# Moving sums of a pooling mixer: VectorE's additions in SBUF, or accumulating transfers in DRAM

## The chip, the cores and the metric

The kernel runs on one core of a Trainium2 chip. A core has TensorE (PE, matrix products; its weight loads are shown as PEld), VectorE (DVE), ScalarE (ACT), GpSimd (POOL) and SyncE (SP), which work from queues of their own and wait for one another by semaphores. SyncE, ScalarE and GpSimd also issue DMA transfers, which sixteen DMA engines carry out. The metric is device microseconds (us) of one execution; lower is better.

## What is computed

The reference is one decoder block on x (1024 tokens x 1024 channels, float32): an RMSNorm and one projection into pooling inputs u, attention's q, k, v, and gates; a multi-scale pooling branch and a sliding-window attention branch, each projected and multiplied by its sigmoid gate, added, projected by W_o, normalised and added to x; and then an MLP with a squared ReLU. What the change touches is the pooling. Its 512 channels are four groups of 128, with windows of 2, 4, 8 and 16 tokens:

```
for gi, w in enumerate((2, 4, 8, 16)):
    c = cs[..., gi * 128:(gi + 1) * 128]          # running sums of u over the tokens
    upper = c[:, 1:]
    lower = jnp.pad(c[:, :S + 1 - w], ((0, 0), (w - 1, 0), (0, 0)))
    count = jnp.minimum(t + 1, w)
    pooled.append((upper - lower) / count)
diff = pooled - u                                  # group by group
mixed = einsum('bsgc,gcd->bsgd', diff, w_pool)
y_pool = mixed * pool_scale
```

So for each token t and channel: the mean of the last w values of u (fewer for the first w - 1 tokens), minus u itself.

## The kernel before

The kernel works in stages, each of which streams weights from DRAM and keeps TensorE at products of 128x128 by 128x512 blocks. Operands are float32, split by a helper (`split`, lines 99 to 104) into a high part (ScalarE's cast, line 101) and a low part (VectorE's subtraction, line 104); each product is three passes over these parts (line 32). The stages in order of time:

1. Projection to q, k, v and attention, block by block of 128 tokens (to about 166 us). In the gaps of the attention's matmuls a generator (`others`, line 633) runs the projection to u. For each group gi, in the order 3, 2, 1, 0, two halves of u are formed (`u_half`, line 591), and u[gi], 128 channels x 1024 tokens, is stored to DRAM (line 611). In the same stage GpSimd makes small tiles for the attention (lines 295 to 330) and, for each of the eight token blocks, two accumulating transfers of the attention's output into DRAM (line 424).
2. Gates (about 166 to 319 us): a Strassen-like scheme of seven block products (class `Pairs`, line 461). In its first part eight pairs of gate weights get two products each (`first` and `second`, lines 847 to 853); weights arrive by line 475, are split by lines 101 and 104, and are multiplied at line 511. Meanwhile the operands for the second part are built from x (`load_x` and `build_gate`, lines 727 to 748). In the second part (line 902) the other products follow and the gates are stored to DRAM.
3. Branches (about 319 to 406 us): first eight calls of `branch` for the attention's projection (line 975), then eight for the pooling's (line 994). Within the first eight, after m = 2, 3, 5 and 6, `pool_part` prepares the pooling groups 1, 0, 2 and 3.
4. W_o (GpSimd's accumulating loads of line 966 add blocks of it), the norms, and the MLP up and down (to the end).

`pool_part(gi)` (line 934) loads u[gi] into an SBUF tile, calls `pool_in` (line 685) and splits the result into the operands `yphi` and `yplo` that the second eight branches multiply. `pool_in` adds the bias on ScalarE (line 688); then VectorE forms the moving sum by doubling: sums over 2 tokens from u and u shifted by one, sums over 4 from those shifted by two, and so on (line 692), with a small copy for the first columns (line 693); 1, 2, 3 and 4 additions for the four groups, each into a further tile of the pool `yy`, which has four buffers. Line 696 forms sum / w minus u, and lines 697 and 698 mend the first w - 1 columns, where the count is smaller.

The order of the work: in the regions `manual_schedule` (lines 755 and 859) the engines that are named there issue in the order of the program; these are TensorE, VectorE and ScalarE, in the second region SyncE too. GpSimd's queue everywhere, and SyncE's outside the second region, are ordered by a scheduler at build time, which lets a later instruction of a queue go ahead of an earlier one when it reckons that the earlier isn't ready. Semaphores are put in by the framework: a transfer that reads what another one wrote waits, in the queue of the engine that issues it, until the other has landed.

Of the kernel before, what the change touches and what calls it, by code (L numbers as in the profile page):

```python
# [8 lines left out]
F32 = mybir.dt.float32  # L9
F32R = mybir.dt.float32r  # L10
AF = mybir.ActivationFunctionType
ALU = mybir.AluOpType
AX = mybir.AxisListType

P = 128
S = 1024
# [5 lines left out]
WINDOWS = (2, 4, 8, 16)  # L22
# [16 lines left out]
C_CNT = C_SIN + NT * 8  # L39
# [3 lines left out]
V_BU = V_G + 8  # L43
# [7 lines left out]
def block_kernel(ctx: ExitStack, tc, xt, x, consts, vecs, sinks, b_qkv, g_post, g_mlp_post,  # L51
                 w_qkv, w_u, w_g, w_pool, w_bp, w_ba, w_o, w_up, w_dn, x1_dram, spill, y_dram, wbp_dram, f_dram, r_dram, out):
    nc = tc.nc
    act, dve, pool, pe = nc.scalar, nc.vector, nc.gpsimd, nc.tensor
# [8 lines left out]
    psum = {"pool": psa_pool.__enter__(), "bufs": {"sc": 1, "at": 3, "mm": 3}}  # L63

    z_dram, u_dram = (spill[i:j] for i, j in ((0, 16), (16, 20)))
    cnt = [0]

    def nm(s):
        cnt[0] += 1
        return f"{s}_{cnt[0]}"  # L70
# [22 lines left out]
    def flat(t):  # L93
        return t.rearrange("p a b -> p (a b)")
# [4 lines left out]
    def split(hi, lo, src, eng=dve, first=None):  # L99
        if first is None:  # L100
            act.copy(hi, src)  # L101
        else:
            first.tensor_copy(hi, src)
        eng.tensor_tensor(lo, src, f32(hi), ALU.subtract)  # L104
# [42 lines left out]
    cst = cp.tile([P, C_N], F32, name="cst")  # L147
    vec = cp.tile([P, V_N], F32, name="vec")
# [533 lines left out]
                return  # L682
            owed[0] -= c

    def pool_in(gi, u, place):

        w = WINDOWS[gi]
        act.activation(u, u, AF.Identity, bias=vec[:, V_BU + gi:V_BU + gi + 1])
        src, step = u, 1
        while step < w:  # L690
            t = place()
            dve.tensor_tensor(t[:, step:], src[:, step:], src[:, :S - step], ALU.add)
            dve.tensor_copy(t[:, :step], src[:, :step])
            src, step = t, 2 * step
            yield
        dve.scalar_tensor_tensor(u[:, w - 1:], src[:, w - 1:], 1.0 / w, u[:, w - 1:], ALU.mult, ALU.subtract)
        dve.tensor_tensor(src[:, :w - 1], src[:, :w - 1], cst[:, C_CNT:C_CNT + w - 1], ALU.mult)
        dve.tensor_tensor(u[:, :w - 1], src[:, :w - 1], u[:, :w - 1], ALU.subtract)
        yield

    def y_place():
        return flat(yy.tile([P, 2, 512], F32, tag="y", name=nm("t")))
# [139 lines left out]

    NG0, NHELD = 8, 6

    def first(p):
# [86 lines left out]
    def pool_part(gi):  # L934
        u = yy.tile([P, S], F32, tag="y", name=nm("d"))
        nc.sync.dma_start(u, u_dram[gi])
        for _ in pool_in(gi, u, y_place):
            pass
        hi = xp.tile([P, S], F32R, tag="x", name=nm("yphi"))
        lo = xp.tile([P, S], F32R, tag="x", name=nm("yplo"))  # L940
        split(hi, lo, u)
        ysp[gi] = hi, lo
# [32 lines left out]
    for m in range(8):  # L975
        branch(w_ba[m], lambda k, hl, th: asp[th][k // 2][hl][:, k % 2, :], 8, m)
        if m == 4:
            sums = wo_load((1, 0), a32, zg[8, 2][1])
            wo_add(sums, (1, 1))
        if m in (2, 3, 5, 6):  # L980
            pool_part({2: 1, 3: 0, 5: 2, 6: 3}[m])
# [363 lines left out]
    def acc4(name):  # L1345
        return [dl.tile([P, 512], F32, tag="acc", name=nm(name), bufs=16) for _ in range(4)]
# [91 lines left out]
    u, v, c11, c12 = acc4("u"), acc4("v"), acc4("c11"), acc4("c12")  # L1438
# [124 lines left out]
```

## Time and profile before

| | us |
|---|---|
| median of 3 runs | 1110.14 (1108.49 to 1111.05) |
| the profiled execution | 1109.43 |
| its span in the trace | 1107.6 |
| TensorE busy | 1097.7 (99%) |
| VectorE busy | 807.1 (73%) |
| ScalarE busy | 547.6 (49%) |
| GpSimd busy | 62.7 (6%) |
| granted TensorE clock | 0.998 |
| DMA, mean over the span | 184 GB/s |

How to read the rows below: L692 is line 692 of the kernel; an arrow `t<-d` means that tile t is written from tile d; `x4` counts instructions. In a view of an engine's instructions in order of time, the first number is the start and the second the length in us, and the brackets at the end hold the idle time before it and what ended that. In a view of waits the numbers are the us in total, the times, and the longest. In a table of stretches come, after the stretch and its length, the busy us of PE, PEld, DVE, ACT and POOL with their instructions, then the granted clock, the mean busy share of the DMA engines, and GB/s. SPq and ACTq are the instructions of SyncE and ScalarE that issue a DMA. Rows of DMA queues give packets, MB and the share of the sixteen engines' time; rows of DMA issues give count, size of one, and us from issue to landing. `spill_dram` is the DRAM tensor that holds the gates (z, 16 slots) and u (4 slots).

### The profile page before, as it was taken

The numbers are of one execution on the slowest core, as the hardware profiler recorded it, in microseconds if no ns is written. First come the engines' busy times: TensorE is split into PE (matmuls) and PEld (weight loads), VectorE is DVE, ScalarE is ACT, GpSimd is POOL, SyncE is SP. The second block draws the span as 40 slices with busy tenths as digits, with TensorE's granted clock in tenths as the row PEclk, the third lists the DMA queues.
The fourth block names the chain that finished last, engine by engine and source line by source line (L and its number), as shares of the span: only waits on it lengthen the run. The fifth ranks groups of instructions, "written<-read, shape, count | busy, mean of one in ns | idle before, by whom it ended". The sixth has DMA issues, their size and how long they took to land.

```text
span 1107.6 us, 13855 instructions
## 1 busy us (share of the span) xinstructions
PE 1097.7 (99%) x5108; PEld 907.5 (82%) x5108; DVE 807.1 (73%) x1175; ACT 547.6 (49%) x916; POOL 62.7 (6%) x107
## 2 busy tenths in 40 slices
PE   9999999999999999999999999999999999999997
PEld 7888788888888888878888888888888888888886
DVE  5578867899768796899878867666548944456596
ACT  7466656444432337587555654444434434344342
POOL 0344220000001120000000000000000000000000
PEclk9999999999999999999999999999999999999999
DMA  9406578355677581570457645445597535534673
GB/s 349 161 11 137 149 169 278 132 191 209 224 256 246 152 186 58 192 271 32 162 197 264 242 169 199 146 151 199 178 371 232 189 98 174 177 102 152 204 229 119
DMA packets 89747, 203.71 MB, mean 184 GB/s; under 512 B 8400, under 2 KB 21072, under 8 KB 89680
## 3 DMA queue, kind: packets, MB, share of 16 engines
q1 hardware_dynamic: 77536, 176.88, 48.0%
q10 hardware_dynamic: 5616, 19.66, 4.6%
q0 software_dynamic: 6528, 6.29, 4.0%
q8 instruction: 40, 0.66, 0.3%
q14 instruction: 27, 0.22, 0.1%
HBM read 147.23 MB, written 55.58 MB: 183 GB/s over the span
## 4 chain that ended last, share of the span: by engine, by line
PE 88%; DVE 5%; DMA 3%; ACT 2%; issue 2%; DVEq 0%; SPq 0%; ACTq 0%
PE mm L511 24%; PE at L511 16%; PE at L1406 16%; PE mm L1406 12%; PE mm L601 4%; PE mm L187 3%; PE mm L445 2%; PE at L196 1%; PE at L419 1%; PE mm L447 1%; PE sc L355 1%; PE sc L187 1%; DMA d<-spill_dram 1%; PE at L1048 1%; PE mm L1048 1%
## 5 line engine op out<-in xcount | busy, mean ns | idle before, releaser
L1406 PE MATMUL at<-ar,wh 128*128 128x512 f32 x744 | 169.6, 389 | 0.0
L1406 PEld LDWEIGHTS at<-ar,wh 128*128 128x128 f32 x744 | 139.6, 188 | 29.3 <-DVE ar L104 0.4
L104 DVE TENSOR_TENSOR wh<-raw,wh 128x1024 fp32r<-128x1024 f32 x53 | 64.8, 1223 | 99.4 <-ACT wh L101 99.4
L1406 PE MATMUL mm<-ar,wh 128*128 128x512 f32 x576 | 131.0, 389 | 0.0
L101 ACT CAST wh<-raw 128x1024 fp32r<-128x1024 f32 x53 | 55.8, 1053 | 146.7 <-PE at L1406 71.6
L1406 PEld LDWEIGHTS mm<-ar,wh 128*128 128x128 f32 x576 | 108.1, 188 | 22.4
L101 ACT CAST wh<-st 128x512 fp32r<-128x512 f32 (+1 forms) x97 | 61.6, 646 | 74.4 <-PE at L511 19.9
L104 DVE TENSOR_TENSOR wh<-st,wh 128x512 fp32r<-128x512 f32 (+1 forms) x97 | 68.8, 719 | 27.8 <-ACT wh L101 25.3
L511 PE MATMUL mm<-gr,wh 128*128 128x512 f32 x333 | 80.4, 391 | 0.0
L511 PEld LDWEIGHTS mm<-gr,wh 128*128 128x128 f32 x333 | 62.1, 188 | 13.1 <-DVE gr L1087 0.4
L511 PE MATMUL mm<-T,wx 128*128 128x512 f32 x288 | 67.6, 389 | 0.0
L511 PEld LDWEIGHTS mm<-T,wx 128*128 128x128 f32 x288 | 54.1, 188 | 11.2
L511 PE MATMUL at<-T,wx 128*128 128x512 f32 x252 | 59.1, 389 | 0.0
L511 PEld LDWEIGHTS at<-T,wx 128*128 128x128 f32 x252 | 47.3, 188 | 9.8
L511 PE MATMUL mm<-x,wh 128*128 128x512 f32 x240 | 55.2, 389 | 0.0
L511 PEld LDWEIGHTS mm<-x,wh 128*128 128x128 f32 x240 | 45.0, 188 | 9.4
L104 DVE TENSOR_TENSOR ar<-B,ar 128x1024 fp32r<-128x1024 f32 x37 | 45.1, 1219 | 4.0 <-ACT ar L101 3.9
L601 PE MATMUL mm<-x,wh 128*128 128x512 f32 x192 | 47.5, 395 | 0.0
L101 ACT CAST ar<-B 128x1024 fp32r<-128x1024 f32 x37 | 38.9, 1051 | 5.9 <-DMA B<-in_w_dn_dram 3.0
L601 PEld LDWEIGHTS mm<-x,wh 128*128 128x128 f32 x192 | 35.3, 188 | 7.7
L511 PE MATMUL at<-gr,wh 128*128 128x512 f32 x150 | 36.7, 390 | 0.0
L101 ACT CAST wx<-ws 128x512 fp32r<-128x512 f32 x30 | 18.6, 620 | 32.7 <-DVE ws L487 17.9
(384 smaller groups left out, 2162.4 us busy)
## 6 DMA issues: line engine op xcount, KB each, us to landing
raw<-f_dram SPq DMA_DIRECT2D x53, 512.0 KB, 3.7
f_dram<-g SPq DMA_DIRECT2D x30, 512.0 KB, 3.3
B<-in_w_dn_dram SPq DMA_DIRECT2D x24, 512.0 KB, 6.3
st<-in_w_up_dram SPq DMA_DIRECT2D x20, 512.0 KB, 4.1
st<-in_w_g_dram SPq DMA_DIRECT2D x18, 512.0 KB, 4.6
f_dram<-g ACTq DMA_DIRECT2D x17, 512.0 KB, 2.6
g<-spill_dram SPq DMA_DIRECT2D x16, 512.0 KB, 5.4
raw<-in_w_dn_dram SPq DMA_DIRECT2D x16, 512.0 KB, 4.7
```

The lines of the kernel that those rows point to most:

```text
L101: act.copy(hi, src)
L104: eng.tensor_tensor(lo, src, f32(hi), ALU.subtract)
L187: pe.matmul(bq, xs_[k][n // 4][:, xh, n % 4 * P:(n % 4 + 1) * P], wq[k][:, h, :], start=k == 0 and j == 0, stop=k == NK - 1 and j == 2)
L196: pe.matmul(bkv_of(n), xs_[k][n // 4][:, xh, n % 4 * P:(n % 4 + 1) * P], wkv[k // 2][:, h, k % 2, :], start=k == 0 and j == 0 and not (joi ...
L355: pe.matmul(sb[:, kv, i, :nk], qt[r, qx, m * P:(m + 1) * P], kx[r, k0:k0 + nk], start=j == 0, stop=j == 2)
L419: pe.matmul(flat(yb), v[:, kv, :], flat(p[:, 4 * kv:4 * kv + 4]), start=j == 0, stop=j == len(mms) - 1)
L445: pe.matmul(bs[th], whi[:, k, :], rhs(k, hl, th), start=k == 0 and hl == 0, stop=False)
L447: pe.matmul(bs[th], wlo[:, k, :], rhs(k, 0, th), start=False, stop=k == nk - 1)
L511: pe.matmul(b, w[:, wh, kt, :], xo[kt][:, xh, :], start=not after and kt == 0 and j == 0, stop=kt == 3 and j == 2, skip_group_check=after)
L601: pe.matmul(b, (whi, wlo)[h][:, k, :], xr(k, xh, th), start=j == 0, stop=j == len(mms) - 1)
L1048: pe.matmul(bs[t], gop[i][kt // 2][gh][:, kt % 2, t * P:(t + 1) * P], wop[i][kt // 2][wh][:, kt % 2], start=not after and kt == 0 and j == ...
L1406: pe.matmul(bs[t], fo[fh][:, k2, t * P:(t + 1) * P], wo_[wh][:, k2, :], start=not after and s2 == 0 and k2 == 0 and j == 0, stop=s2 == NS ...
```

## The change

The moving sums are formed in DRAM. The DRAM tensor gets ten more slots of 128 x 1024, one for each doubling step of each group. Ahead of the gates' stage in the program, `window_sums` issues for every step and group, in GpSimd's queue, a copy of the source (u, or the sum of the step before) into the new slot, and an accumulating transfer that adds the same source to it, shifted by 1, 2, 4 or 8 tokens. `pool_part` loads u and the finished sum. Since the sums are now of u without its bias, `pool_in` scales the first w - 1 columns by w / count (VectorE), then takes sum / w + bias (ScalarE) and subtracts u + bias (VectorE).

```diff
+    sum_dram = [[spill[20 + gi * (gi + 1) // 2 + i] for i in range(gi + 1)] for gi in range(4)]
...
-    def pool_in(gi, u, place):
-
-        w = WINDOWS[gi]
-        act.activation(u, u, AF.Identity, bias=vec[:, V_BU + gi:V_BU + gi + 1])
-        src, step = u, 1
-        while step < w:
-            t = place()
-            dve.tensor_tensor(t[:, step:], src[:, step:], src[:, :S - step], ALU.add)
-            dve.tensor_copy(t[:, :step], src[:, :step])
-            src, step = t, 2 * step
-            yield
-        dve.scalar_tensor_tensor(u[:, w - 1:], src[:, w - 1:], 1.0 / w, u[:, w - 1:], ALU.mult, ALU.subtract)
-        dve.tensor_tensor(src[:, :w - 1], src[:, :w - 1], cst[:, C_CNT:C_CNT + w - 1], ALU.mult)
-        dve.tensor_tensor(u[:, :w - 1], src[:, :w - 1], u[:, :w - 1], ALU.subtract)
-        yield
+    def window_sums(step):
+
+        for gi in (1, 0, 2, 3):
+            if 1 << step < WINDOWS[gi]:
+                src, dst = (sum_dram[gi][step - 1] if step else u_dram[gi]), sum_dram[gi][step]
+                pool.dma_start(dst, src)
+                pool.dma_start(dst[:, 1 << step:], src[:, :S - (1 << step)], accum_op=ALU.add)
+
+    def pool_in(gi, u, t):
+
+        w, bias = WINDOWS[gi], vec[:, V_BU + gi:V_BU + gi + 1]
+        act.activation(u, u, AF.Identity, bias=bias)
+        edge = t[:, :w - 1]
+        dve.scalar_tensor_tensor(edge, edge, float(w), cst[:, C_CNT:C_CNT + w - 1], ALU.mult, ALU.mult)
+        act.activation(t, t, AF.Identity, bias=bias, scale=1.0 / w)
+        dve.tensor_tensor(u, t, u, ALU.subtract)
...
+    for step in range(4):
+        window_sums(step)
+
     NG0, NHELD = 8, 6
...
         nc.sync.dma_start(u, u_dram[gi])
-        for _ in pool_in(gi, u, y_place):
-            pass
+        t = y_place()
+        nc.sync.dma_start(t, sum_dram[gi][-1])
+        pool_in(gi, u, t)
...
-    spill = nc.dram_tensor("spill_dram", (20, P, S), F32, kind="Internal").ap()
+    spill = nc.dram_tensor("spill_dram", (30, P, S), F32, kind="Internal").ap()
```

## The prediction

> **What bounds the kernel now.** I read the page's header first, then the busy time of each engine by stage, then what TensorE waited for.
>
> ```profile
> span 1107.6 us, 13855 instructions
> ...
> PE 1097.7 (99%) x5108; PEld 907.5 (82%) x5108; DVE 807.1 (73%) x1175; ACT 547.6 (49%) x916; POOL 62.7 (6%) x107
> ```
>
> ```profile
> 0.00:20.00 20.00, 18.47 (x89) 15.21 (x90) 10.88 (x21) 13.93 (x25) 0.20 (x4) 1.00 0.88 327
> ...
> 110.00:215.00 105.00, 104.89 (x515) 85.05 (x512) 81.17 (x122) 60.41 (x140) 13.76 (x19) 1.00 0.64 173
> 215.00:320.00 105.00, 105.00 (x464) 86.91 (x463) 87.78 (x131) 45.51 (x59) 0.00 (x0) 1.00 0.65 218
> 320.00:360.00 40.00, 40.00 (x178) 33.11 (x177) 33.92 (x56) 12.03 (x14) 4.16 (x4) 1.00 0.80 259
> 360.00:420.00 60.00, 59.85 (x264) 49.13 (x263) 50.97 (x57) 22.33 (x27) 11.97 (x10) 1.00 0.65 156
> ...
> 1090.00:1108.00 18.00, 10.71 (x48) 8.54 (x46) 10.76 (x32) 2.95 (x9) 0.00 (x0) 0.88 0.31 117
> ```
>
> ```profile
> PEld mm L445 <- ACT wh L101: 0.5, 1, 0.5
> PEld at L511 <- DVE gr L104: 0.5, 1, 0.5
> ```
>
> The columns of the second fence are the stretch, its length, busy time (instructions) of PE, PEld, DVE, ACT and POOL, the granted clock, the DMA share and GB/s. TensorE is idle for 1107.6 - 1097.7 = 9.9 us in all, and 1.5 + 7.3 of that lie at the two ends. From 215 to 360 us, which holds the whole pooling stage, it is idle for 0.00 us, and from 360 to 420 for 0.15. The clock is 1.00 wherever it counts. So the kernel is bound by TensorE, and the other engines show in the time only where they make TensorE wait. The longest such waits around the change are 0.5 us.
>
> **What the change takes away.** The rows of the removed work, and of the operation that ScalarE gets once more for each group:
>
> ```profile
> L692 DVE TENSOR_TENSOR t<-t x6: 1206/1220/1225, 322.4 to 354.7; 128x1022 f32<-128x1022 f32 x3, 128x1020 f32<-128x1020 f32 x2, 128x1016 f32<-128x1016 f32 x1
> L692 DVE TENSOR_TENSOR t<-d x4: 1218/1224/1225, 314.4 to 346.8; 128x1023 f32<-128x1023 f32 x4
> ...
> L688 ACT ACTIVATE d<-d,vec x4: 1150/1152/1153, 313.2 to 345.6; 128x1024 f32<-128x1024 f32 x4
> ```
>
> Ten additions of 1.22 us leave VectorE: 12.2 us, and some small copies with them. The final subtraction stays, in another form. ScalarE gains 4 x 1.15 = 4.6 us, at 12.03 us busy of 40: hidden by its own idle time. VectorE's 12.2 us lie between 314 and 358 us, where TensorE is never idle, so taking them away is worth between 0 and the 0.15 us that TensorE loses after 360. I take 0: the cover is TensorE's own stream, which has no gap to close.
>
> **What it adds.** Ten copies and ten accumulating transfers from DRAM to DRAM, about 512 KB each, in GpSimd's queue, and four loads of 512 KB in SyncE's. An accumulation may go only when its copy has landed, and the next copy of the same group only when the accumulation has; GpSimd waits for each in its own queue. Two questions decide: do the sums come in time, and whom do they disturb?
>
> *In time?* GpSimd's queue, its price for a DMA, and the first and the last of the loads that will need the sums:
>
> ```profile
> 169.38 2.04 POOL L424 DMA_DIRECT2D y_dram<-yt  x2 [9.37 <-ACT qkv L736]
> 350.47 1.72 POOL L959 COPY s<-g 128x1 f32<-128x1 f32 x2 [179.06 <-DVE t L693]
> ```
>
> ```profile
> L966 POOL DMA_DIRECT2D s<-in_w_o_dram x8 | 9.7, 1262 | 15.1 <-DMA s<-in_w_o_dram 7.6 <-DVE wh L104 3.6 <-DVE wo L104 2.1
> ```
>
> ```profile
> s<-in_w_o_dram POOLq DMA_DIRECT2D x8, 512.0 KB, 7.3
> ...
> spill_dram<-u SPq DMA_DIRECT2D x4, 512.0 KB, 3.9
> ```
>
> ```profile
> 308.80 0.33 SPq L936 DMA_DIRECT2D d<-spill_dram  x1
> ...
> 341.47 0.33 SPq L936 DMA_DIRECT2D d<-spill_dram  x1
> ```
>
> GpSimd is free from 171.4 to 350.5 us. No DMA from DRAM to DRAM is in this trace. The nearest rows are the accumulating loads of W_o (1.26 us on GpSimd, 7.3 us to landing), and the store of u (3.9 us) as the low end for a copy. If all twenty ran strictly one after the other from 171.4, each at 1.26 + 7.3 = 8.56 us, the last would land at 171.4 + 171 = 343 us, just after the last group's load goes out now. With the copies at 3.9 it is 309 us. A following copy belongs to another group in most places and needn't wait for the accumulation ahead of it, so it is earlier still. Against lateness there is a little more room behind: these three rows (the third is a piece of the chain of waits, 192 matmuls in 43.52 us) say how much.
>
> ```profile
> 359.13 1.23 DVE L104 TENSOR_TENSOR yplo<-d,yphi 128x1024 fp32r<-128x1024 f32 x1
> ```
>
> ```profile
> 318.89 0.39 PE L445 MATMUL mm<-yahi,wh 128*128 128x512 f32 x1
> ```
>
> ```profile
> 166.30 43.52 PE mm L511 x192
> ```
>
> The last group is ready at 359.13 + 1.23 = 360.4 us. A branch is 24 matmuls of 43.52 / 192 = 0.227 us, so TensorE comes to the second eight branches at 318.89 + 8 x 5.44 = 362.4, and to that group's rows, the last quarter, 4.1 us later. So I take the sums to be in time. The Trainium skill's page "DMA: Bandwidth & Descriptors" (Anatomy of one DMA, SWDGE path) fits 2.0 us plus the bytes at 436 GB/s, 3.2 us for such a transfer; by it, an estimate, the strictly serial chain would be done at 171.4 + 20 x 4.46 = 261 us. The trace's 7.3 us is more than twice that and decides here.
>
> *Whom do they disturb?* First, when they run. GpSimd isn't in the lists of engines with a hand-written order, so the scheduler may place the sums in any gap after u is stored. SyncE shows that it does such things:
>
> ```profile
> 113.49 0.33 SPq L611 DMA_DIRECT2D spill_dram<-u  x1
> ...
> 158.72 0.33 SPq L475 DMA_DIRECT2D st<-in_w_g_dram  x1
> ...
> 163.98 0.33 SPq L475 DMA_DIRECT2D st<-in_w_g_dram  x1
> ...
> 167.62 0.53 SPq L611 DMA_DIRECT2D spill_dram<-u  x1
> ...
> 170.71 0.95 SPq L475 DMA_DIRECT2D st<-in_w_g_dram  x1
> ```
>
> The fourth and last u is written in the program before gate 4 and gate 6 are loaded (the third and fourth L475), yet both loads go out ahead of it. I therefore expect the sums of group 3 from about 113.5 + 3.9 = 117 us on, and the others as their u lands. Now the DMA engines (the last two columns are share and GB/s):
>
> ```profile
> 160.00:170.00 10.00, 10.00 (x46) 8.27 (x45) 7.86 (x12) 5.75 (x10) 0.63 (x3) 1.00 1.02 262
> 170.00:180.00 10.00, 10.00 (x46) 8.29 (x45) 6.62 (x10) 4.80 (x10) 1.41 (x2) 1.00 1.08 313
> 180.00:190.00 10.00, 10.00 (x46) 8.29 (x45) 8.93 (x14) 6.42 (x12) 0.00 (x0) 1.00 0.74 290
> 190.00:200.00 10.00, 10.00 (x46) 8.29 (x45) 8.16 (x14) 5.85 (x10) 0.00 (x0) 1.00 0.32 107
> ```
>
> From 160 to about 184 us they are full before anything is added. What a transfer takes of them comes from the shares of two queues: ScalarE's 16 stores in 215 to 320, and GpSimd's 8 accumulations in 320 to 420:
>
> ```profile
> q10 hardware_dynamic: 2304, 8.39, 21.2%
> ```
>
> ```profile
> q0 software_dynamic: 2176, 4.19, 24.7%
> ```
>
> A plain 512 KB is 0.212 x 105 / 16 = 1.4 us of all 16 engines, an accumulated one 0.247 x 100 / 8 = 3.1 us. A pair is 4.5 us, the ten pairs 45 us. The four extra loads later are 4 x 1.4 us at 0.80 share, with no TensorE wait near them: nothing.
>
> In the full stretch the gate weights come just in time:
>
> ```profile
> 179.39 0.62 ACT L101 CAST wh<-st 128x512 fp32r<-128x512 f32 x1 [3.59 <-DMA st<-in_w_g_dram]
> ```
>
> ```profile
> 180.04 0.69 DVE L104 TENSOR_TENSOR wh<-st,wh 128x512 fp32r<-128x512 f32 x1 [1.53 <-ACT wh L101]
> ```
>
> This is gate 8, loaded at 170.71 and landed at 179.3, 8.6 us later. TensorE's 192 matmuls from 166.30 are sixteen blocks of 2.72 us; gate 8's is the seventh, so it starts at 166.30 + 6 x 2.72 = 182.6, and needs the low part two matmuls later, at 183.1. That part is ready at 180.7. The load may be 2.4 us later; beyond that, each us is one of TensorE's, and TensorE never gets it back. From 160.7 to 179.3 (18.6 us) one chain of pairs, each some 15 us long (two landings of 7.3), takes 4.5 / 15 = 0.30 of the engines: 5.6 us of delay for the loads behind, so 5.6 - 2.4 = **3.2 us of stall**. Bounds: if the sums start only at 171.4, a single copy (1.4 us) lies ahead of the landing, and the stall is 0; if two groups' chains run at once they take 0.5 to 0.6 of the engines, 9.3 us at 0.5, and the stall is 6.9. I take the middle one, because GpSimd waits in order for each landing, which keeps the chains mostly apart. The additions' 0 and the sums' 3.2 make the sum.
>
> Three rows of the DMA queues and issues from 160 to 190 us:
>
> ```profile
> q1 hardware_dynamic: 4493, 8.12, 78.3%
> q0 software_dynamic: 1050, 0.51, 16.1%
> ...
> xr<-in_xt_dram SPq DMA_DIRECT2D x4, 512.0 KB, 9.4
> ```
>
> GpSimd's queue q0 already has a sixth of the engines there, with 0.51 MB in small packets, beside SyncE's q1. The Trainium skill's page "DMA: Bandwidth & Descriptors" (Queues, rings and completion order) says that each DMA engine takes turns between queues packet by packet. By that rule GpSimd's queue would get up to half while it has work, the 6.9 us end. These rows, with q0 not always at work, neither show nor exclude the half.
>
> **The rivals.** (1) *No stall, no change.* The scheduler keeps the sums behind the attention's last transfer, or SyncE's queue isn't slowed enough: 1.4 us of delay against 2.4 us of slack. For it: TensorE rides over landings of 8.6 us already. Against it: SyncE's early loads. Time: 1110.1. (2) *Two chains at once,* with the half share: 6.9 us, 1117. For it: the groups' u come 18 us apart, about a pair's length. (3) *The sums are late.* SyncE then stands at the load of a sum, with the branch weights and gates queued behind it, and TensorE starves. It decides once a DRAM-to-DRAM transfer costs more than 8.56 us in series from 171.4; at the 9.4 us that the x loads take in the full stretch, 20 x 10.66 = 213 us end at 385, 43 us after the last load goes now, and about 37 us of stall less what overlaps: some 20, 1130. Against it: most copies overlap, and the start is early. (4) *Faster by more than 0.2%.* VectorE would have to hold TensorE somewhere after 360 that the waits don't show; at most 0.15 us is there, and only a luckier order downstream gives 2.2 us: 1107.5.
>
> **How the numbers follow.** The three runs span 2.6 us; about 0.2%, 2.2 us, is what a measurement of this kernel can tell from no change. The profiled execution took 1109.43 us for its span of 1107.6; plus 3.2 that is 1112.6. The runs' median is 0.7 above it, so 1113.3. Chances: forecast 0.42, rival (1) 0.38, (2) 0.10, (3) 0.05, (4) 0.05. The range goes from rival (1), less about 1 us of scatter (1109), to rival (2) and 3 us beyond it, for a stall in a second place (1120); it leaves out (3) and (4). The forecast's own range is 1112.4 to 1115. Slower 0.42 + 0.10 + 0.05 = 0.57, same 0.38, faster 0.05.
>
> **What would show it.** Right: GpSimd's DMAs of the sums between 117 and 230 us, some of them ahead of the attention's last accumulation; gate 8's or a neighbour's load landing 10 us or more after its issue; a wait of PEld on L511 for ScalarE's or VectorE's cast near 183, of about 3 us, and everything behind it shifted by as much; VectorE some 13 us less busy with no TensorE gap closed. Wrong: TensorE at 105.0 busy from 110 to 215 again (rival 1); SyncE waiting on a sum's transfer near 310 to 345 (rival 3); or a TensorE gap in a stage that I called covered.

## The result, and the profile after

| | before | after |
|---|---|---|
| median | 1109.85 us of 4 runs (1108.49 to 1111.05) | 1117.99 us of 4 runs (1117.43 to 1119.47) |
| span of the profiled execution | 1107.6 | 1116.2 |
| granted clock, mean | 0.998 | 0.995 |

The kernel is slower: ratio 1.0076, 95% interval 1.0058 to 1.0093. The forecast was 1113.3, its range 1109 to 1120. The gates are counted as in the prediction. Lines of the code have moved: L511 is L512, L475 is L476, L101 and L104 are L102 and L105; the sums' copies are L691, their accumulations L692.

The header and the busy times of the page after:

```profile
span 1116.2 us, 13878 instructions
...
PE 1100.2 (99%) x5108; PEld 909.6 (81%) x5108; DVE 795.4 (71%) x1151; ACT 551.7 (49%) x920; POOL 75.6 (7%) x127
```

VectorE is 11.7 us less busy and GpSimd 12.9 us more, and the span is 8.6 us longer. Where these arose, the waits of TensorE say (us in total, times, longest):

```profile
PE mm L512 <- ACT wh L102: 4.9, 1, 4.9
...
PE mm L622 <- DVE u L610: 0.6, 1, 0.6
PE mm L512 <- DVE g L540: 0.3, 1, 0.3
```

The two rows left out stand at the start and in the attention, as before. The first one is new, a single wait. Its place, in TensorE's instructions in order of time, and ScalarE's casts of gate weights around it:

```profile
187.76 6.51 PE L512 MATMUL mm<-x,wh 128*128 128x512 f32 x28
199.20 18.88 PE L512 MATMUL mm<-x,wh 128*128 128x512 f32 x72 [4.92 <-ACT wh L102]
```

```profile
179.09 0.62 ACT L102 CAST wh<-st 128x512 fp32r<-128x512 f32 x1 [2.51 <-DMA st<-in_w_g_dram]
187.06 0.62 ACT L102 CAST wh<-st 128x512 fp32r<-128x512 f32 x1 [4.21 <-DMA st<-in_w_g_dram]
198.53 0.62 ACT L102 CAST wh<-st 128x512 fp32r<-128x512 f32 x1 [7.75 <-DMA st<-in_w_g_dram]
```

These are gates 8, 10 and 12. Gate 8 is on time (its cast starts at 179.09; before, at 179.39). Gate 12 is not, and the chain of waits, in order of time, shows its load:

```profile
179.31 19.19 DMA st<-in_w_g_dram
198.50 0.02 issue
198.53 0.63 ACT wh L102
```

The load went out at 179.31 and landed 19.2 us later. In the kernel before, it went out at 178.53 and landed 8.5 us later, and the same cast is the second of these two, so it started at about 188.5:

```profile
187.94 1.14 ACT L101 CAST wh<-st 128x512 fp32r<-128x512 f32 x2
```

TensorE comes to that weight at 194.28 (199.20 less 4.92). For that the cast, with its 0.63 us and the 0.04 behind it, would have had to start by 193.6. So the load had about 5 us in hand, was 10 us late, and 4.9 us were left. Beside it worked the sums. GpSimd's instructions in order of time:

```profile
160.19 1.18 POOL L691 DMA_DIRECT2D spill_dram<-spill_dram  x1
170.48 2.06 POOL L425 DMA_DIRECT2D y_dram<-yt  x2 [9.11 <-ACT z L519]
174.84 0.53 POOL L691 DMA_DIRECT2D spill_dram<-spill_dram  x1 [2.31 <-DMA spill_dram<-u]
175.42 1.66 POOL L692 DMA_DIRECT2D spill_dram<-spill_dram  x2
185.37 0.81 POOL L692 DMA_DIRECT2D spill_dram<-spill_dram  x1 [8.30 <-DMA spill_dram<-spill_dram]
...
226.03 0.81 POOL L692 DMA_DIRECT2D spill_dram<-spill_dram  x1 [4.99 <-DMA spill_dram<-spill_dram]
```

Five of the twenty transfers went out by 160.2, from 116.9 us on. Then GpSimd's queue stood at an accumulation of the attention (L425) that waited for its data, and after it for the last u. The other fifteen follow from 174.84 on: three of them within 2.3 us, and then each as an earlier one lands, several side by side. The DMA queues from 179 to 199 us, the life of gate 12's load (packets, MB, share of the sixteen engines), first after, then before:

```profile
q0 software_dynamic: 757, 3.25, 62.0%
q1 hardware_dynamic: 916, 3.32, 43.2%
```

```profile
q1 hardware_dynamic: 1154, 4.21, 55.7%
q0 software_dynamic: 14, 0.00, 0.2%
```

GpSimd's q0 held more of the engines than SyncE's q1 with its loads, and moved as many bytes.

One more thing lies behind the wait. TensorE in steps of 2 us (stretch, length, busy, granted clock, DMA share, GB/s):

```profile
194.00:196.00 2.00, 0.27 (x2) 1.00 1.04 395
196.00:198.00 2.00, 0.00 (x0) 0.81 0.96 406
198.00:200.00 2.00, 0.80 (x2) 0.50 1.11 393
200.00:202.00 2.00, 2.00 (x6) 0.50 0.90 190
202.00:204.00 2.00, 2.00 (x6) 0.50 1.11 219
204.00:206.00 2.00, 2.00 (x10) 0.98 1.04 192
```

The granted clock fell to 0.50 during the wait and stayed there until 4.8 us after it. Seventy-two matmuls took 18.88 us; at the 0.227 us of the undisturbed stream, with the last one's 0.39, they take 16.5. That is 2.4 us more. Not all of it is the clock's: in a run below (the one with nine copies) the same 72 take 17.15 us behind a shorter wait, at a clock of 1.00, so that some 1.7 of the 2.4 are left for the clock. The account: TensorE reaches the gates' stage at 167.07 instead of 166.30 (0.8), waits 4.9, loses 2.4 behind the wait, and 0.3 in the last wait of the list, which lies between 500 and 600 us: 8.4 of the 8.6 us. The first branch matmul starts at 327.20 instead of 318.89, 8.3 later, and from there on the kernel keeps that distance.

### The profile page after: what moved, and what is told of

It reads as the page before. It is cut to its first block, busy times and chain, and to the rows that moved or that the text cites. A ratio compares the mean times of both kernels' runs of the same rounds, so it can differ in the third digit from the quotient of the medians.

```text
span 1116.2 us, 13878 instructions
## 1 busy us (share of the span) xinstructions
PE 1100.2 (99%) x5108; PEld 909.6 (81%) x5108; DVE 795.4 (71%) x1151; ACT 551.7 (49%) x920; POOL 75.6 (7%) x127
## 4 chain that ended last, share of the span: by engine, by line
PE 85%; DVE 8%; DMA 3%; ACT 2%; issue 2%; DVEq 0%; ACTq 0%; SPq 0%
PE mm L512 22%; PE at L1412 16%; PE at L512 15%; PE mm L1412 12%; PE mm L446 5%; PE mm L188 3%; PE mm L448 3%; PE mm L602 2%; DMA st<-in_w_g_dram 2%; PE at L197 1%; PE sc L188 1%; PE at L1054 1%; PE mm L1054 1%; PE at L420 1%; PE sc L356 1%
## 5 line engine op out<-in xcount | busy, mean ns | idle before, releaser
L105 DVE TENSOR_TENSOR wh<-raw,wh 128x1024 fp32r<-128x1024 f32 x53 | 64.8, 1223 | 99.3 <-ACT wh L102 99.3
L102 ACT CAST wh<-raw 128x1024 fp32r<-128x1024 f32 x53 | 55.8, 1052 | 146.7 <-PE at L1412 71.7
L102 ACT CAST wh<-st 128x512 fp32r<-128x512 f32 (+1 forms) x97 | 61.7, 645 | 85.2 <-PE at L512 20.7
L105 DVE TENSOR_TENSOR wh<-st,wh 128x512 fp32r<-128x512 f32 (+1 forms) x97 | 69.1, 720 | 31.2 <-ACT wh L102 28.8
L512 PE MATMUL mm<-gr,wh 128*128 128x512 f32 x333 | 80.1, 391 | 0.0
L512 PEld LDWEIGHTS mm<-gr,wh 128*128 128x128 f32 x333 | 62.1, 188 | 12.8
L512 PE MATMUL mm<-T,wx 128*128 128x512 f32 x288 | 67.5, 389 | 0.0
L512 PEld LDWEIGHTS mm<-T,wx 128*128 128x128 f32 x288 | 54.1, 188 | 11.2
L512 PE MATMUL mm<-x,wh 128*128 128x512 f32 x240 | 57.8, 401 | 4.9 <-ACT wh L102 4.9
L512 PE MATMUL at<-T,wx 128*128 128x512 f32 x252 | 59.1, 389 | 0.0
L512 PEld LDWEIGHTS mm<-x,wh 128*128 128x128 f32 x240 | 46.6, 195 | 15.3 <-ACT wh L102 5.3
L512 PEld LDWEIGHTS at<-T,wx 128*128 128x128 f32 x252 | 47.3, 188 | 9.8
L602 PE MATMUL mm<-x,wh 128*128 128x512 f32 x192 | 47.5, 395 | 0.0
L105 DVE TENSOR_TENSOR ar<-B,ar 128x1024 fp32r<-128x1024 f32 x37 | 45.1, 1219 | 3.2 <-ACT ar L102 3.1
L102 ACT CAST ar<-B 128x1024 fp32r<-128x1024 f32 x37 | 38.9, 1051 | 5.0 <-DVE B L1387 2.8
L512 PE MATMUL at<-gr,wh 128*128 128x512 f32 x150 | 36.6, 390 | 0.0
L512 PE MATMUL at<-T,wh 128*128 128x512 f32 x138 | 34.6, 391 | 0.0
```

The source lines that it names most:

```text
L512: pe.matmul(b, w[:, wh, kt, :], xo[kt][:, xh, :], start=not after and kt == 0 and j == 0, stop=kt == 3 and j == 2, skip_group_check=after)
L602: pe.matmul(b, (whi, wlo)[h][:, k, :], xr(k, xh, th), start=j == 0, stop=j == len(mms) - 1)
```

## The experiments

The theory: the whole loss comes from the transfers' hold on the DMA engines while the gates' weights are loaded, with a clock fall behind the wait; the relief of VectorE is worth nothing. The rivals: the change's other edits cost something; it is one load's place that matters; or the number of DMA starts, not the bytes.

**The traffic alone.** To the kernel before, the new slots and `window_sums` are added; `pool_part` stays as it was, and the sums are read by nobody.

```diff
+    sum_dram = [[spill[20 + gi * (gi + 1) // 2 + i] for i in range(gi + 1)] for gi in range(4)]
...
+    for step in range(4):
+        window_sums(step)
```

> The kernel before, with the sums' twenty transfers issued as in the change and never read; VectorE still makes the sums. Theory: the transfers alone do the harm, so TensorE stands 4 to 6 us near 194 with a low clock behind it, and the time is 1116 to 1119. Rival A (the harm comes from the changed pool_part): 1110. If the removal of VectorE's work is worth something after all, this kernel is slower than the changed one by that much; I expect 0 to 0.5 us.

Measured: 1118.37 us, ratio 1.0080 (1.0065 to 1.0095), the same as the whole change. TensorE's wait for gate 12's cast is 6.0 us here:

```profile
199.91 19.50 PE L512 MATMUL mm<-x,wh 128*128 128x512 f32 x72 [6.03 <-ACT wh L102]
```

and its 72 matmuls behind the wait take 19.50 us, 0.6 more than those of the whole change.

**The relief alone.** After without the twenty transfers; the "sum" that is loaded is u once more.

```diff
-    for step in range(4):
-        window_sums(step)
...
-        nc.sync.dma_start(t, sum_dram[gi][-1])
+        nc.sync.dma_start(t, u_dram[gi])
```

> The changed kernel without the twenty transfers: pool_part loads u a second time in place of the sum (so the pooling's values are not the sums), and does everything else as in the change. Theory: VectorE's 12 us lie under TensorE's stream, so the time is that of the kernel before, 1109 to 1110.5, with no TensorE wait over 0.6 us between 130 and 800. Rival A: over 1115. Rival C (VectorE's relief is worth something): below 1108.

Measured: 1110.43 us, ratio 1.0011 (1.0001 to 1.0020). VectorE's busy time falls from 807.1 to 794.8 us and the time does not. So with the rest of this kernel as it stands, sums that cost nothing would bring nothing, and a better place for the transfers could at best take the loss away.

**The same bytes, copied instead of accumulated.**

```diff
-                pool.dma_start(dst[:, 1 << step:], src[:, :S - (1 << step)], accum_op=ALU.add)
+                pool.dma_start(dst[:, 1 << step:], src[:, :S - (1 << step)])
```

> The changed kernel with the ten accumulating transfers made plain copies of the same rows (so the slots do not hold the sums): as many transfers, bytes written and waits in GpSimd's queue, but no reading of the destination. Theory (occupation of the DMA engines): 20 x 1.4 = 28 us of all engines instead of 45; the load of gate 12 lands in about 13 us instead of 19, TensorE stands 0 to 1.5 us near 194, and the time is 1110 to 1112.5. Rival D (the number of transfers and packets decides, not what each occupies): the stall stays at 4 to 6 us, 1116 to 1119.

Measured: 1114.36 us (1112.47 to 1116.44), ratio 1.0049 (1.0030 to 1.0068), between the two expectations and in neither. The q0 row of the whole page, before, after and here:

```profile
q0 software_dynamic: 6528, 6.29, 4.0%
```

```profile
q0 software_dynamic: 8288, 16.77, 7.8%
```

```profile
q0 software_dynamic: 7648, 16.77, 6.5%
```

Twenty transfers take 7.8% of 1116.2 less 4.0% of 1107.6, 42.8 us of all engines; as plain copies 6.5% of 1112.0 less the same 44.3, 28.0 us. Here, too, fifteen starts go out in the stretch of the harm (174.49 to 216.36 us; after, 174.84 to 226.03). From 174 to 234 us q0 moves the same bytes, but holds less of the engines (after, then here):

```profile
q0 software_dynamic: 2032, 8.11, 58.8%
```

```profile
q0 software_dynamic: 1438, 8.11, 37.5%
```

TensorE's wait shrinks to 2.2 us, and the clock stays at 1.00. So neither the starts nor the bytes alone set the loss; it falls with what the transfers hold of the engines. Whether their time or their packets count, which are fewer too, isn't separated.

```profile
196.42 9.90 PE L512 MATMUL mm<-x,wh 128*128 128x512 f32 x40 [2.17 <-ACT wh L102]
```

**An eighth of the bytes.** The traffic-only kernel with 16 of 128 partitions in each transfer.

```diff
-                pool.dma_start(dst, src)
-                pool.dma_start(dst[:, 1 << step:], src[:, :S - (1 << step)], accum_op=ALU.add)
+                pool.dma_start(dst[:16], src[:16])
+                pool.dma_start(dst[:16, 1 << step:], src[:16, :S - (1 << step)], accum_op=ALU.add)
```

> The kernel before with the 20 transfers beside VectorE's own additions, as in the run with the traffic alone, but each transfer takes 16 of the 128 partitions: 64 KB instead of 512 KB, 1.3 MB in all instead of 10.5; what they write is read by nobody. Same number of DMA starts, of waits in GpSimd's queue and of instructions. Theory (the bytes that occupy the DMA engines beside the gates' weights are the harm): the wait at 194 us goes to under 1 us, and the time is 1110 to 1111 us. Rival (the DMA starts themselves, GpSimd's work for them or the sharing of the queues): at least half of the loss stays, 1114 to 1118 us.

Measured: 1110.42 us of 12 runs, ratio 1.0006 (0.9996 to 1.0015). The loss is gone with as many starts in all. Gate 10's cast, which the kernel after starts at 187.06, starts at 183.70 (before, at 183.26), and TensorE has no gap from 160 to 210:

```profile
183.70 0.62 ACT L102 CAST wh<-st 128x512 fp32r<-128x512 f32 x1 [1.23 <-DMA st<-in_w_g_dram]
```

```profile
160.00:210.00 50.00, 50.00 (x222) 1.00 0.73 224
```

The doses stand in line: 0.1% at 6.6 us of all engines (q0 4.6% of 1107.0 here, less 44.3), 0.5% at 28.0, 0.8% at 42.8. But this run changes the times too. Small transfers land sooner, nothing piles up, and eighteen of the twenty have gone out by 170.34:

```profile
170.34 0.76 POOL L692 DMA_DIRECT2D spill_dram<-spill_dram  x1 [2.66 <-DMA spill_dram<-spill_dram]
```

So by itself it shows only that twenty starts, most of them ahead of the gates, do no harm. That starts among the gates' loads are not the harm either rests on the plain copies, which keep them.

**A wait without traffic.** Into the kernel before, GpSimd copies are put that hold the tile of gate 12's weights, so that its cast is late; nine and thirteen of them. No DMA is added.

```diff
+            if self.src is w_g and (p, i) == (6, 1):
+                with tc.manual_schedule(engines={mybir.EngineType.Pool}):
+                    for _ in range(13):
+                        pool.tensor_copy(flat(t[:, 0]), self.f0[4][:, 512:])
```

> The kernel before, with no transfer added: nine copies on GpSimd, each 128 x 512 from the result of the fifth gate block, into the tile that ScalarE's cast of gate 12 then overwrites, so that the cast waits for them. It measures by itself what a wait of TensorE at that place costs. The nine copies take some 8 to 11 us from 186, so TensorE stands 0 to 4 us at 194. Theory (a wait is followed by a stretch at half clock, which costs as much again as half of it lasts): with a wait over 3 us the granted clock falls to 0.5 for some 5 us and the time is the wait plus 2 to 3 us above the kernel before; below 2.3 us, as in the run with plain copies, the clock stays. Rival (the low clock came from the sums' transfers or from heat): the clock stays at 1.00 however long TensorE waits.

> The same with thirteen copies, 12 to 16 us from 186: TensorE stands 4 to 9 us at 194, and by the theory 5 us of half clock follow, so that it loses 2 to 3 us more than it waited; by the rival, the wait alone is lost.

Measured, in a single execution each: nine copies make a wait of 1.44 us and 1112.76 us, with the clock at 1.00 behind it. Thirteen make 4.14 us and 1115.6, and here the clock falls although no transfer was added (nine first, then thirteen):

```profile
195.40 17.15 PE L515 MATMUL mm<-x,wh 128*128 128x512 f32 x72 [1.44 <-ACT wh L101]
```

```profile
197.97 18.83 PE L515 MATMUL mm<-x,wh 128*128 128x512 f32 x72 [4.14 <-ACT wh L101]
```

```profile
196.00:198.00 2.00, 0.03 (x1) 0.50 0.00 0
198.00:200.00 2.00, 2.00 (x5) 0.50 0.00 0
200.00:202.00 2.00, 2.00 (x7) 0.50 0.00 0
```

With thirteen, the same 72 matmuls take 18.83 us, as in the kernel after, with the DMA engines at 0.00. So the slow matmuls after the wait come of the wait, not of the transfers. With nine they take 17.15 at a full clock, 0.7 more than undisturbed: TensorE's weight loads wait there for VectorE's low parts, 0.43 us at 196.12 and 0.37 at 201.83.

**The hit load ahead of the crowd.** After, with gate 12 loaded earlier, before the last pair of x, into a tile of its own.

```diff
-            if p == 1:
+            if p == 0:
+                gt.load(10)
+                gt.load(12, g32([NK, P]))
+            elif p == 1:
...
-            if p + 5 < NG0:
-                gt.load(2 * p + 10)
-            elif p < 5:
+            if p == 2:
+                gt.load(14)
+            if 2 < p < 5:
```

> The changed kernel, sums as in the change, with the load of gate 12 put ahead of the last pair of x loads in SyncE's order, into a tile that is free at once; the x loads are needed only at about 202 us. Nothing is left out. Theory (the 4.9 us at 194 are the latency of that one load, 19 us against 15 of lead, so lead cures it without taking a transfer away): gate 12 lands by 190, no gap over 1 us at 194, and the time is 1110 to 1113; a new gap of up to 2 us near 205 (gate 14 or the x loads) is possible. Rival A (the loss isn't tied to this load: GpSimd's waits, or bandwidth that some other load then lacks): 1115 or more.

Measured: 1119.07 us, ratio 1.0085 (1.0068 to 1.0102). A miss. The wait at 194 us is gone, but another takes its place in the second part of the gates, with its own clock fall:

```profile
189.70 11.44 PE L512 MATMUL mm<-x,wh 128*128 128x512 f32 x48 [0.34 <-ACT wh L102]
228.67 4.44 PE L512 MATMUL at<-x,wh 128*128 128x512 f32 x12 [4.59 <-ACT ar L102]
```

The thing that is late here isn't a load. The chain of waits leads to a store of z, which ScalarE issues at 217.74 and which lands 8.8 us later (the two such stores of the kernel before land in 2.6 and 3.7); VectorE can write that tile again only then:

```profile
226.64 0.69 DVE L540 TENSOR_TENSOR z<-z,at 128x512 f32<-128x512 f32 x1 [5.33 <-DMA spill_dram<-z]
```

So it is not one load's place. While the sums run (the last goes out at 229 us), the transfer with the least time in hand is late, load or store; take one away and another is.

**Group by group.** After, with all steps of one group emitted before the next group's.

```diff
-        for gi in (1, 0, 2, 3):
+        for gi, step in ((gi, step) for gi in (1, 0, 2, 3) for step in range(4)):
```

> The kernel after with the sums emitted group by group, all steps of one group before the next group, so that GpSimd's queue, which waits at every step for the transfer before, has one transfer in flight and seldom two, instead of the steps of four groups side by side. Bytes, number of transfers and VectorE's work are as after. Theory (what matters is how large a share of the DMA engines the sums hold while a gate's weights are loaded): with the fixed time of each start between two transfers the share falls and the sums end later; the wait at 194 us falls under 2.5 us, too short for the clock to fall, and the time is 1111 to 1115 us. Rival (only the total of bytes in the stretch counts, wherever the wait then stands): 1117 to 1119 us, with about 5 us of waits and a clock fall.

Measured: 1119.85 us, ratio 1.0092 (1.0079 to 1.0105). This told nothing of its question: GpSimd's starts went out at the same places and, within 1.3 us, at the same times as after (first 117.1, three from 175.0 on, last 226.0). The order in which the program names the steps is not the order in the queue. Whether one transfer at a time would be gentler stays open.

**The sums late.** After, with the sums emitted behind the gates' first part; a marker, one GpSimd copy of a column that is ready at about 192 us, keeps them from running earlier.

```diff
+    with tc.manual_schedule(engines={mybir.EngineType.Pool}):
+        pool.tensor_copy(small(1, "mark"), gt.f0[5][:, 512:513])
+        for step in range(4):
+            window_sums(step)
```

> The changed kernel with one edit: a one-column copy on GpSimd, which reads the result of the sixth gate block (written near 191 us), stands ahead of all the sums, and the sums then go out in the order of the program. Nothing is left out; only the start moves, from 117 to about 191 us, behind the full stretch of the DMA engines. Theory (the sums' transfers delay the load of gate 12, TensorE stands 4.9 us at 194 and then runs 6 us at half clock): both are gone, the load lands within 6 us, and the time is that of the kernel before plus 0 to 2 us (1110 to 1112), the 2 for the gate load near 242 that has no slack and would now meet the sums. Rival A (the new pool_part, its loads and the order after it cost the time): still 1116 to 1119. Rival B (the sums come late when they start here): a wait of SyncE on a sum's transfer near 317 to 345 and TensorE idle behind 360, over 1115.

Measured: 1140.53 us, ratio 1.0282 (1.0267 to 1.0298). A large miss. From 110 to 215 us TensorE now runs undisturbed (104.94 of 105), but in the second part of the gates there are waits of 2.53 and 3.21 us, each with a clock fall (behind the first stands the same store of z, which takes 6.9 us), and the last accumulation goes out at 360 us:

```profile
359.71 0.64 POOL L966 COPY s<-g 128x1 f32<-128x1 f32 x2 [84.29 <-DVE g L938]
360.29 0.80 POOL L692 DMA_DIRECT2D spill_dram<-spill_dram  x1
```

GpSimd's queue runs in order, and the scheduler had put two copies for W_o ahead of that accumulation; they waited 84 us for VectorE. At 381 us TensorE waits another 2.43 us for an operand of the pooling, again with a clock fall. So that order was the first suspect.

**Late, with GpSimd's queue in program order** up to the end of the branches; otherwise the same.

```diff
+    order_pool = tc.manual_schedule(engines={mybir.EngineType.Pool})
+    order_pool.__enter__()
...
+    order_pool.__exit__(None, None, None)
```

> The late start again, and now GpSimd's queue keeps the order of the program up to the end of the branches; in the run before, the last of the twenty was put behind two copies that wait for the fifth attention branch, went out at 360 us instead of about 281, and SyncE stood for it at 368. Theory (that run's 31 us are two gaps of 2.5 and 3.2 us with half clock behind them in the gates' stage, and the rest the late sum): the last sum lands near 290, TensorE has no gap of over 0.6 us behind 320, and the time is 1116 to 1120: the gates' loads meet the sums' transfers wherever these run. Rival A (the late sum was a consequence of the slow transfers, not of the queue): still over 1130. Rival B (the gaps in the gates' stage came by chance of the schedule): 1110 to 1112.

Measured: 1141.45 us, ratio 1.0283 (1.0265 to 1.0301). A miss too: the last accumulation goes out at 286.8 and the wait at 381 is gone, but the second part of the gates now has waits of 3.96, 3.10 and 1.75 us, and nothing is won. The engines from 800 to 900 us, where the sums have long ended, in the kernel before (columns as in the prediction's table of stretches):

```profile
800.00:900.00 100.00, 100.00 (x443) 82.81 (x442) 71.06 (x63) 41.94 (x46) 0.00 (x0) 1.00 0.71 239
```

And here, with the second part of the gates, for which the prediction has the row of before (464 matmuls, 105.00 us):

```profile
215.00:320.00 105.00, 95.30 (x391) 75.79 (x390) 78.61 (x119) 40.03 (x55) 10.11 (x15) 0.95 0.84 255
...
800.00:900.00 100.00, 100.00 (x431) 80.67 (x430) 66.30 (x64) 40.16 (x44) 0.00 (x0) 1.00 0.74 258
```

Two losses, then. From 215 to 320, gaps and a low clock. And from 800 to 900 TensorE is busy all the time at a clock of 1.00, and yet does 431 matmuls where it did 443. Both late kernels have this, the kernel after has not. Is it the sums, or the marker that only these two have?

**The marker alone**, in the kernel before.

```diff
+    with tc.manual_schedule(engines={mybir.EngineType.Pool}):
+        pool.tensor_copy(small(1, "mark"), gt.f0[5][:, 512:513])
```

> The kernel before and nothing else but the marker that held the sums back in the two late runs: one GpSimd copy of a column into a new tile of 4 bytes in each partition; the sums are VectorE's again, and no transfer is added. In the late runs every matmul of the MLP took longer at a granted clock of 1.00 (the 744 matmuls at<-ar,wh 174.3 us in all where the kernel before has 169.6, one 395 ns where it has 389), and some 14 us of their 31 were lost after 430 us, when the sums had long ended. Theory: the new tile is to blame, since it shifts the place in SBUF of all that is allocated behind it, and the sums have no part in this. Then this run takes 1110 + 13 to 15 = about 1124 us, with the 744 matmuls at 174 us. Rival: it is an after-effect of the sums or of the two clock falls, and this run takes 1110 us with 169.6.

Measured: 1126.22 us, ratio 1.0149 (1.0136 to 1.0162). It is the marker. The largest group of matmuls of the MLP, before and here (busy us, mean ns of one):

```profile
L1406 PE MATMUL at<-ar,wh 128*128 128x512 f32 x744 | 169.6, 389 | 0.0
```

```profile
L1408 PE MATMUL at<-ar,wh 128*128 128x512 f32 x744 | 174.4, 396 | 0.0
```

No gap, no wait and a full clock, and yet these matmuls keep TensorE busy 2.8% longer.

**Late and in program order, with a marker of 64 bytes** in each partition instead of 4.

```diff
-    pool.tensor_copy(small(1, "mark"), gt.f0[5][:, 512:513])
+    pool.tensor_copy(small(16, "mark")[:, :1], gt.f0[5][:, 512:513])
```

> The late run with GpSimd's queue in program order, the marker's tile 64 bytes in each partition instead of 4; the order of every engine's instructions is the same. Theory (the 4-byte tile shifts what lies behind it in SBUF): the 744 matmuls are back at about 170 us, the 13 us after 430 us go, and what is left is the 17.6 us that the kernel lost up to the MLP, less what slower matmuls cost ahead of it: 1124 to 1128 us. That is still far above the kernel after, so late sums are worse than early ones. Rival (the sums' after-effect): 1141 us as before.

Measured: 1137.85 us (1136.20 to 1144.37), ratio 1.0268 (1.0241 to 1.0295), and the 744 matmuls stay at 174.4 us. A miss: the width of the marker's tile is not what slows them. What in the marker does (the place of the tiles behind it, or the schedule around it) stays open. What can be said is the price of late sums beside the marker's own, if that is the same in all four kernels: 1140.53, 1141.45 and 1137.85 are 14.3, 15.2 and 11.6 us above the 1126.22 of the marker alone. The change with early sums costs 8.1. Most of that price is lost before the branches: their first matmul starts at 331.07, 336.68 and 333.28, where with the marker alone it starts at 321.70. So holding the sums until the attention is over moves the harm to the second part of the gates and makes it larger.

## Why the prediction was right, and where it was not

- *VectorE's 12.2 us are worth 0.* Right: the relief alone gives 1.0011.
- *The sums come in time.* Right: the last accumulation goes out at 226.0, and TensorE runs 50.00 of 50 us from 320 to 370.
- *The scheduler runs them early, some ahead of the attention's last accumulation.* Right, for five of twenty. The other fifteen came behind it, as rival (1) had it, and the stall came all the same.
- *A pair costs 4.5 us of all engines, the ten pairs 45.* Right: 42.8.
- *A gate's load is delayed beyond its slack, and TensorE never gets it back.* Right as a mechanism: the traffic alone brings the whole loss, and the plain copies, with as many starts and bytes in the same stretch but less of the engines, bring 2.2 us of wait for 4.9. Wrong in place: the prediction looked at gate 8, which was loaded at 171.5, ahead of the fifteen, and landed on time. Gate 12, loaded among them, was hit; it had about 5 us in hand, not gate 8's 2.4.
- *One chain at a time takes 0.30 of the engines, so 5.6 us of delay and 3.2 us of stall.* This step failed. "GpSimd waits in order for each landing, which keeps the chains mostly apart" does not hold: three transfers that had queued up behind L425 went out within 2.3 us and others while they were under way, q0 held 62.0% in gate 12's 20 us beside q1's 43.2%, and the cast came 10 us late. That is the case of rival (2), whose half share gave 9.3 us of delay. The sum had a second flaw: it counts the delay from 160.7, which stands in no row. Over the 8.6 us of gate 8's own load the same 0.30 makes 2.6 us, which leaves 0.2 us of stall. The rule that the prediction weighed there from the Trainium skill's page "DMA: Bandwidth & Descriptors" (Queues, rings and completion order), turns packet by packet, fits better than the 0.30: from 180 to 190 us, with transfers of both in flight throughout, the two queues had nearly equal packets and bytes.

```profile
q0 software_dynamic: 430, 1.56, 65.8%
q1 hardware_dynamic: 424, 1.54, 40.9%
```

- *Each us beyond the slack is one us of TensorE's.* Too low: what a wait costs beyond itself was in no term of the sum. It is 2.4 us here and 2.3 in the run with thirteen copies, which added no DMA; some 1.7 of that is the clock's fall, since the run with nine copies lost 0.7 without one.
- *Nothing ahead of the gates.* The 0.8 us by which TensorE is late at 167 were not foreseen. Of these, 0.2 are there ahead of the first transfer (an attention matmul that started at 102.30 starts at 102.49), and nearly all the rest is the wait for u at 128.40, the second row of waits above. It is not clear that the transfers make it: TensorE starts the gates 0.4 us late with an eighth of the bytes and 0.5 us late without any transfer, in the relief alone.

The time lies within the range because rival (2) was in it, outside the forecast's own 1112.4 to 1115: 4.9 for 3.2, plus 2.4 and 0.8. That rival (2)'s 1117 comes so near is partly luck: it has 6.9 us of wait, 2.0 too many, and nothing for what follows a wait.

## What to carry to other kernels

Work taken off an engine that TensorE never waits for is worth nothing, and the bytes that replace it are paid for on a shared resource. Before transfers are added beside a stream of weights, list every load and store in their stretch with its time in hand, count the added queue as an equal partner of the loads' queue and not by its mean share, and look for the wait that lets its transfers pile up; here, moving the one load that was hit only showed the next transfer. A marker or a dummy instruction in an experiment needs its own control run: here it cost twice what the change did.

## What was not expected of the hardware

**The clock after a wait.** The runs above hold seventeen waits of TensorE between 1.4 and 6.1 us behind the start of the kernel. Behind those of 1.44, 1.75, 1.87, 2.08, 2.17 and 3.55 us the granted clock stayed at 1.00; behind those of 1.98, 2.43, 2.53, 3.10, 3.21, 3.42, 3.96, 4.14, 4.59, 4.92 and 6.03 us it fell to 0.50 for a few us. So from 3.96 on it always fell, below 1.9 never, and between it went either way. The Trainium skill's page "TensorE: Matmul & The Clock Gate" (What's actually happening) says that the clock is halved after an idle window of some 3.4 us that runs freely, whenever the idle time begins. That the same length goes either way agrees; falls after 1.98, 2.43 and 2.53 us, shorter than that window, do not.

**Matmuls of one shape at two speeds.** At a granted clock of 1.00 and without a gap, 884 matmuls in 800 to 1000 us became 859 through one GpSimd copy into a new tile, which ran at 193 us. The cause was not found.
